# Every on-chip tile at a multiple of 128 bytes, in a kernel of two transformer blocks

## The chip, the cores and the metric

The kernel runs on one core of one Trainium2 chip. Times are device microseconds of one launch, the median of several runs. The core has TensorE (PE, matmuls and weight loads), VectorE (DVE), ScalarE (ACT), GpSimd (POOL) and SyncE (SP, which here issues the large loads), and an on-chip memory, SBUF, of 128 partitions. A tile occupies the same byte range of every partition, so "where a tile starts" is one number, its offset within a partition.

## The reference

Two blocks in a row on 272 tokens (16 meta tokens and 256) of width 2048, all in float32. What counts for the matmuls:

```
first block, x: 272 tokens
    proj = rms(h) @ w_in                           # 2048 -> rwkv, attention and gate columns
    y_a = rwkv7(...)    y_b = attention(...)       # 16 heads of 64 each, 1024 wide
    h = h + (g_a*(y_a@w_a) + g_b*(y_b@w_b)) @ w_o  # g: sigmoid of the gate columns
    gate, up = rms(h) @ w_gate_up                  # 5632 each
    h = h + (silu(gate)*up) @ w_down
second block, 256 tokens
    proj = rms(h) @ w_in_2
    y_hyena = x0 * long_conv(x1*v, filters)    y_attn = latent_attention(...)   # 1024 wide each
    h = h + rms([rms(y_hyena), rms(y_attn)] @ w_out)
    g, u = rms(h) @ w_up                           # 5632 each
    h = h + rms((gelu(conv3(g)) * u) @ w_down_2)
```

Past the mixer of the first block only the 256 real tokens are needed. The kernel multiplies transposed: weights are the stationary 128x128 block, and the tokens, 256 or 272 columns, the moving side.

## The kernel before

To keep float32 accuracy each float32 operand is split into two float32r parts, high and low, and each block product is three matmuls into one PSUM bank: high by high, low by high, high by low (`mm3`). `stream` brings a matrix in pieces of eight 128x128 blocks (512 KB): SP loads a piece to `wr`, ScalarE copies it to `wh` (L191), VectorE makes `wl = wr - wh` (L192). `wr`, `wh` and `wl` have three buffers each. `dense` then runs over the reduction steps k, with one piece in use and the next ones in preparation:

```
    def mm3(self, out, wh, wl, xh, xl, start, stop):
        nc.tensor.matmul(out, lhsT=wh, rhs=xh, start=start, stop=False)     # L209
        nc.tensor.matmul(out, lhsT=wl, rhs=xh, start=False, stop=False)     # L210
        nc.tensor.matmul(out, lhsT=wh, rhs=xl, start=False, stop=stop)      # L211

    def tl(self, pool, shape, tag, dt=F32, bufs=None):
        self.n += 1
        kw = {} if bufs is None else {"bufs": bufs}
        return pool.tile(list(shape), dt, tag=tag, name=f"{tag}_{self.n}", **kw)
```

The order of the work is the program's order, with the loads and splits of the weights brought forward; no instruction's place depends on addresses. The stages, and the moving side of each: w_in (tiles `xh`, `xl`: 16 rows of 272 tokens, 1088 bytes a row) with the heads' scans and attention between its blocks; w_ab (`ya`, `yb`); w_o (`mh`, `ml`); w_gu (`x2h`, `x2l`), 88 blocks of outputs by 16 steps; w_down (`hh`, `hl`), 16 blocks by 44 steps; the projections of the second mixer (`x3h`, `x3l`); w_out (`yhh`, `yhl`, `yah2`, `yal2`); w_up2 (`x4h`, `x4l`), 88 by 16; w_down2 (`hh2`, `hl2`), 16 by 44. All but w_in move 256 columns, rows of 1024 bytes.

All tiles come from pools that grow from the left end of a partition, or, with `side="right"`, from the right end down, each tile as long as its data. A pool opened first lies outermost. The left side begins with `g` (the columns of constants, `cols`, `con`, the token norms `R`, the sums `acc`) and `small` (the temporaries `rs_v`, `rs_r`, `rs_q`, `ssq`), then the weights; behind them the stage's input (`x2`, `x3`, `x4`, and in the first stage `xh`). On the right lie `h`, `mh`, then `hh`, and in the second block `yhh` and its like, then `hh2`.

Starts in bytes, as the program places them (one tile of each kind), and what is left over modulo 256:

```
tile                        before           after
wr, wh, wl (9 buffers)      28448 ...  32    28672 ...   0
x2h, x3h, x4h               65312      32    65536       0
x2l, x3l, x4l               81696      32    81920       0
xh (row k: + 1088 k)       106912     160   107520       0
mh                         180192     224   180096     128
hh, hh2                    122848,139232 224  (-96)    128
yhh                        194528     224   194432     128
rs_r, rs_q (mod 128)                 64, 0             0, 0
```

Buffers of the weights are 4096 bytes apart and their blocks 512, so all weights have the same remainder. Before, every SBUF tile starts at a multiple of 32 bytes, and 294 of 4267 at a multiple of 128.

Of the kernel before, what the change touches and what calls it, by code (L numbers as in the profile page):

```python
# [31 lines left out]
PIECE = 8  # L32

# [23 lines left out]
def in_order():  # L57
    """The column blocks of the first projection in the order in which they are computed."""
    out = [("wf", 0), ("ad", 0), ("gd", 0), ("gd", 1)]
    g = 0  # L60
    for j in range(9):
        if j < 8:
            out += [("k", j), ("v", j), ("r", j)]
        if j:
            out += [("fk", j - 1), ("fq", j - 1), ("fv", j - 1)]
        for _ in range(GATES_PER_PAIR[j]):
            out.append(("g", g))
            g += 1
    return out + [("g", i) for i in range(g, 32)]
# [18 lines left out]
def shape_constants():  # L88
    """Constants that depend on shapes alone."""
    p = np.arange(P)  # L90
    half = p // 64

    def pack(at, n, **vs):
        c = np.zeros((P, n), np.float32)
        for k, v in vs.items():
            s, w = at[k]
            c[:, s : s + w] = np.asarray(v, np.float32).reshape(P, w)
        return c

    z30 = np.zeros((P, 30))  # L100
    z30[p, 14 + half] = 1.0
    con = pack(CON, NCON, ident=np.eye(P), ones=np.ones((P, P)),
               bo=half[:, None] == half[None, :], i64=np.concatenate([np.eye(64)] * 2), z30=z30,
               eps=np.tile([[1e-6, 64e-5]], (P, 1)))

    s = np.arange(64)[:, None]
    t = np.arange(64)[None, :]
    g = np.stack([s < t, s <= t], 1)
    lv = np.stack([(s // (2 * b) == t // (2 * b)) & (s % (2 * b) < b) & (t % (2 * b) >= b)
                   for b in (1, 2, 4, 8, 16)], 1)  # L110
    sc = np.ones((P, L))
    sc[:, ::64] = 0.0
    crw = pack(CRW, NCRW, gmask=np.concatenate([g, g]), lev=np.concatenate([lv, lv]), scan=sc)

    ca = [np.where(np.arange(T)[None, :] > p[:, None] + NM + P * b, BIG, 0.0) for b in range(2)]
    cfx = pack(CFX, NCFX, caus=np.stack(ca, 1))

    pm = np.zeros((P, P))
    pm[half * 64 + (p + 32) % 64, p] = 1.0
    inv = (1.0 / (10000.0 ** (np.arange(0, 64, 2, dtype=np.float32) / np.float32(64)))).astype(np.float32)  # L120
    ang = (np.arange(S, dtype=np.float32)[:, None] * inv[None, :]).astype(np.float64)
    co, si = np.cos(ang).T, np.sin(ang).T
    cml = pack(CML, NCML, perm=pm, cos=np.concatenate([co] * 4), sin=np.concatenate([-si, si] * 2))

    n = 2 * S
    tt = np.arange(S, dtype=np.float64)
    ff = np.arange(S, dtype=np.float64)
    ph = 2.0 * np.pi * ((tt[:, None] * ff[None, :]) % n) / n
    alt = np.where(np.arange(S) % 2 == 0, 1.0, -1.0)
    re, im = np.cos(ph), -np.sin(ph)  # L130
    im[:, 0] = alt
    dft = np.concatenate([re, im], 1).reshape(2, P, 2 * S).transpose(1, 0, 2)
    ire, iim = np.cos(ph).T * (2.0 / n), -np.sin(ph).T * (2.0 / n)
    ire[0] /= 2.0
    iim[0] = alt / n
    idft = np.concatenate([ire, iim], 0).reshape(4, P, S).transpose(1, 0, 2)
    chy = pack(CHY, NCHY, dft=dft, idft=idft)

    f32 = np.float32
    pos = np.linspace(0.0, 1.0, S, dtype=f32)  # L140
    wv = (f32(2.0 * math.pi) * np.arange(S, dtype=f32) / f32(S)).astype(f32)
    fr = np.linspace(1e-4, 15, 16, dtype=f32)
    ang = (wv[:, None] * fr[None, :]).astype(f32)
    zp = np.concatenate([pos[:, None], np.cos(ang), -np.sin(ang)], 1).T
    dl = np.abs(np.linspace(math.log(1e-2) / 1.5, math.log(1e-2) / 0.3, 1024, dtype=f32))
    win = np.exp(-pos[:, None] * dl[None, :]) + f32(0.05)
    cfi = pack(CFI, NCFI, zpos=np.pad(zp, ((0, P - 33), (0, 0))), win=win.reshape(2, P, 1024).transpose(1, 0, 2))
    return {"con": con, "crw": crw, "cfx": cfx, "cml": cml, "chy": chy, "cfi": cfi}


class Builder:
    def __init__(self, nc, tc, a, o, upto, ctx):
        self.nc, self.tc, self.a, self.o, self.upto, self.ctx = nc, tc, a, o, upto, ctx
        self.n = 0
        self.nbank = 0
        self.banks = "dabc"
        self.pending = {}

# [9 lines left out]
    def tl(self, pool, shape, tag, dt=F32, bufs=None):  # L168
        self.n += 1
        kw = {} if bufs is None else {"bufs": bufs}  # L170
        return pool.tile(list(shape), dt, tag=tag, name=f"{tag}_{self.n}", **kw)
# [22 lines left out]
    def weights(self, src, kt, pools=None, size=PIECE, tag="w"):  # L194
        """Bring [128, kt, 128] weights on chip and split them into two float32r parts."""
# [10 lines left out]
    def mm3(self, out, wh, wl, xh, xl, start, stop):  # L206
        """out (PSUM) += (wh + wl)^T (xh + xl) without the product of the two low parts' last bits."""
# [5 lines left out]
    def stream(self, name):  # L213
        """The blocks [128, 128] of a matrix in the order of their use, PIECE at a time."""
# [6 lines left out]
    def dense(self, out, st, kt, xh, xl, tok):  # L221
        """out (PSUM) = sum over kt of w[p, kt, m]^T x[p, kt, tok]."""
# [4 lines left out]
    def group(self, out, st, kt, xh, xl, toks, bring):  # L227
        """Several blocks of outputs side by side: each block of x is used as soon as it is there."""
# [6 lines left out]
    def bank(self):  # L235
        """A bank for a block of outputs while no other work needs banks."""
# [3 lines left out]
    def gained(self, src, gain, hi, lo):  # L240
        """hi + lo = src * gain (a value for every partition)."""
# [3 lines left out]
    def sumsq(self, acc, src, first):  # L245
        """acc (+)= src^2, but for the last one added, which total() adds."""
# [10 lines left out]
    def total(self, acc, n=S):  # L257
        """The sums over the partitions of acc, on every partition (PSUM)."""
# [7 lines left out]
    def headsum(self, ps, w, src, n, pool=None):  # L266
        """ps = the sums of src over the 64 partitions of each head, weighted by w (exact in float32r)."""
# [7 lines left out]
    def warm_rsqrt(self, src):  # L275
        """Has the table of the reciprocal square root loaded ahead of its use."""
# [3 lines left out]
    def rstd(self, out, ss, n, scale, eps, floor=None, pool=None):  # L280
        """out = (scale * ss + eps)^-1/2 (ss in PSUM), refined by one Newton step."""
# [16 lines left out]
    def run(self):  # L298
        nc, tc, a, ctx = self.nc, self.tc, self.a, self.ctx
        g = self.g = self.pool(ctx, "g")  # L300
        self.small = self.pool(ctx, "small", 1)
# [88 lines left out]
    def residual(self, i, ps, gain, xh, xl):  # L390
        """h += ps; the next layer's input (but for the norm of each token) and its sum of squares."""
# [5 lines left out]
    def fox_setup(self, pr):  # L397
# [9 lines left out]
        # cumulative log forget gates  # L407
# [9 lines left out]
        # for each head of a pair: the high parts of the 16 heads' sums (and 16 unused rows), then the low ones  # L417
# [56 lines left out]
    def headnorm(self, ps, t0, w, w2, tag, gain):  # L474
        """RMS norm of each head (64 partitions) of ps * R."""
# [13 lines left out]
    def softmax(self, sc, mx, sign, w2):  # L489
        """sc = exp(sign * sc + mx) / its sum over the row, in place."""  # L490
# [63 lines left out]
    def conv3(self, ps, taps, bias, R, w2, tag):  # L554
        """Centred 3-tap convolution over the tokens of ps * R, plus bias."""
# [11 lines left out]
    def phase_mix(self, xh, xl, ys, rs):  # L567
# [3 lines left out]
        with ExitStack() as c:  # L571
            w = self.pool(c, "pmx")
            w2 = self.pool(c, "pmx2", 2)
# [21 lines left out]
            # latents of the queries and of the keys and values  # L595
# [22 lines left out]
            # queries [nope | rope], keys, and values (token-major) of all heads  # L618
# [61 lines left out]
    def transforms(self, w, jobs):  # L680
        """Split constant transform matrices into two float32r parts."""
# [5 lines left out]
    def filters(self, c):  # L687
        """The spectra of the implicit filters, in DRAM: a generator of steps."""
# [36 lines left out]
        for quarter in range(4):  # L725
# [17 lines left out]
            # [re 0, re 1, im 0, im 1, re 0 with the Nyquist term in its first row]  # L743
# [170 lines left out]
    def phase_x(self, pa):  # L914
# [4 lines left out]
        with ExitStack() as ph:  # L919
# [14 lines left out]
            # keep the tensor engine's clock up until the first data is there  # L934
# [6 lines left out]
            # the four blocks of the low-rank inputs and of the forget gates, while x comes in  # L941
# [20 lines left out]
    def lerp(self, ps, mu, t0, t1, out):  # L962
        """out = z + (z_prev - z) * mu for tokens t1.. of z = ps * R (ps holds tokens t0..)."""
# [11 lines left out]
    def phase_heads(self):  # L975
        """Projections of the first layer, its two kinds of heads, and the gates."""
# [4 lines left out]
        with ExitStack() as pr:  # L981
# [23 lines left out]
            # decay, rate and gate lora inputs  # L1005
# [43 lines left out]
    def rwkv_pair(self, j, w):  # L1049
# [7 lines left out]
        # decay exponents and rate  # L1057
# [13 lines left out]
        # the four scaled operands  # L1071
# [19 lines left out]
        # bonus term  # L1091
# [5 lines left out]
        # Gram blocks: rows (B s | K s), columns (A t | R t)  # L1097
# [15 lines left out]
        # values and (B | K) scaled to the end of the chunk, token-major  # L1113
# [19 lines left out]
        # X = (I - L)^-1 by doubling the size of the inverted diagonal blocks  # L1133
# [16 lines left out]
        for lv in range(1, 5):  # L1150
            # the first chunk has but 16 tokens
# [37 lines left out]
        # chunk after chunk  # L1189
# [33 lines left out]
        # group norm, bonus and gate  # L1223
# [21 lines left out]
def tiles_of(w):  # L1245
    """[K, M] -> [M / 128, 128, K / 128, 128], contiguous for every block of 128 columns."""
# [4 lines left out]
def stream_of(blocks):  # L1251
    """[n, KT, 128, 128] blocks in the order of their use -> [pieces, 128, PIECE, 128]."""
    return np.ascontiguousarray(blocks.reshape(-1, PIECE, P, P).transpose(0, 2, 1, 3))


def blocks_of(w):
    """[K, M] -> [M / 128, K / 128, 128, 128]"""
# [108 lines left out]
```

## Time and profile before

| | us |
|---|---|
| median of 3 runs | 2909.88 |
| lowest, highest | 2907.11, 2911.15 |
| profiled execution: span | 2911.4 |
| TensorE busy | 2864.9 (98%) |
| VectorE, ScalarE, GpSimd busy | 1863.8, 1337.1, 209.8 |
| mean granted TensorE clock | 0.993 |

The page gives the profiled execution its span alone; it lies 1.5 us above the median of the runs, which were taken apart from it, so the span is used as its time. In rows of groups, `out<-in` are the program's tiles, then partitions x elements, the count, the busy time and the mean of one in ns, and the idle time ahead with what ended it; a bank of PSUM is `psa` to `psd`, and the blocks of outputs go round the four, so a stage's matmuls stand in four times three rows. In rows of windows, stretch and length are followed by TensorE's busy time and its count of matmuls, the granted clock, and the DMA's share and rate. In rows of the timeline, the first column is the start and the second the duration in us.

### The profile page before, as it was taken

The page shows a single profiled execution, that of the slowest core. Times are in us where ns is not written, and L with a number is a line of the kernel's source. Part 1 is how long each engine was busy: PE and PEld are TensorE (multiplying, and loading weights), DVE is VectorE, ACT ScalarE, POOL GpSimd, SP SyncE. Part 2 cuts the span into 40 slices and gives each one's busy share as a digit, 9 for nine tenths or more (in the row PEclk, how much of TensorE's full clock was granted, in tenths as well). Part 3 has the DMA queues.
Part 4 walks back from the last instruction along what each step waited for, and adds up shares of the span by engine and source line. Part 5 has one row for each costly group of instructions (what it writes and reads, how often), then busy time and mean ns, then how long its engine had stood idle before and what let it go on. Part 6 is the DMA issues. An engine that isn't in the chain of part 4 may idle for free.

```text
span 2911.4 us, 58350 instructions
## 1 busy us (share of the span) xinstructions
PE 2864.9 (98%) x24314; PEld 2745.4 (94%) x24314; DVE 1863.8 (64%) x2958; ACT 1337.1 (46%) x1990; POOL 209.8 (7%) x358
## 2 busy tenths in 40 slices
PE   8999999999999999999999999999989999999997
PEld 7988888888989999999999999999989999999997
DVE  8856666766566655555555556687686666665445
ACT  6545555555434444444444445444454444444442
POOL 4000010000000200000000000010220000000001
PEclk9999999999999999999999999999999999999998
DMA  6433333334676555555556666444656655656664
GB/s 208 137 109 111 106 113 101 114 110 134 200 232 198 183 181 182 186 183 181 183 186 198 202 203 214 155 146 143 196 174 184 184 183 183 183 185 217 194 192 143
DMA packets 147481, 496.32 MB, mean 170 GB/s; under 512 B 16208, under 2 KB 30800, under 8 KB 146768
## 3 DMA queue, kind: packets, MB, share of 16 engines
q1 hardware_dynamic: 129024, 459.46, 50.2%
q10 hardware_dynamic: 17552, 31.03, 3.2%
q8 instruction: 190, 3.11, 0.4%
q0 software_dynamic: 640, 2.10, 0.2%
q14 instruction: 75, 0.61, 0.1%
HBM read 477.32 MB, written 15.20 MB: 169 GB/s over the span
## 4 chain that ended last, share of the span: by engine, by line
PE 96%; DVE 2%; DMA 1%; ACT 1%; issue 0%; SPq 0%; ACTq 0%; POOL 0%; DVEq 0%
PE psd L211 13%; PE psd L210 13%; PE psd L209 13%; PE psb L209 5%; PE psb L211 5%; PE psa L211 5%; PE psc L210 5%; PE psb L210 5%; PE psa L210 5%; PE psc L209 5%; PE psc L211 5%; PE psa L209 5%; PE psa L1107 1%; PE psa L1158 1%; PE psa L1164 1%; DMA fw<-filt_dram 1%
## 5 line engine op out<-in xcount | busy, mean ns | idle before, releaser
L192 DVE TENSOR_TENSOR wl<-wr,wh 128x1024 fp32r<-128x1024 f32 (+1 forms) x872 | 1066.6, 1224 | 665.0 <-ACT wh L191 664.0
L191 ACT CAST wh<-wr 128x1024 fp32r<-128x1024 f32 (+1 forms) x872 | 909.1, 1043 | 1256.5 <-PE psd L211 382.4
L210 PE MATMUL psd<-xh,wl 128*128 128x256 f32 (+2 forms) x1280 | 371.5, 290 | 0.0
L211 PE MATMUL psd<-xl,wh 128*128 128x256 f32 (+2 forms) x1280 | 371.4, 290 | 0.0
L209 PE MATMUL psd<-xh,wh 128*128 128x256 f32 (+2 forms) x1280 | 369.9, 289 | 0.6 <-DVE p L969 0.6
L209 PEld LDWEIGHTS psd<-xh,wh 128*128 128x128 f32 x1280 | 241.2, 188 | 8.6 <-issue 4.1
L211 PEld LDWEIGHTS psd<-xl,wh 128*128 128x128 f32 x1280 | 241.1, 188 | 7.8 <-issue 3.2
L210 PEld LDWEIGHTS psd<-xh,wl 128*128 128x128 f32 x1280 | 240.9, 188 | 5.3 <-issue 0.2
L252 POOL TENSOR_TENSOR acc<-acc,ssq 128x256 f32<-128x256 f32 x70 | 89.2, 1274 | 1103.8 <-ACT ssq L254 1103.7
L211 PE MATMUL psd<-x3l,wh 128*128 128x256 f32 x496 | 142.4, 287 | 0.0
L209 PE MATMUL psd<-x3h,wh 128*128 128x256 f32 x496 | 142.4, 287 | 0.0
L210 PE MATMUL psd<-x3h,wl 128*128 128x256 f32 x496 | 140.8, 284 | 0.0
L209 PE MATMUL psa<-x4h,wh 128*128 128x256 f32 x352 | 100.2, 285 | 3.8 <-ACT x4h L242 3.8
L210 PE MATMUL psa<-x4h,wl 128*128 128x256 f32 x352 | 100.4, 285 | 2.8 <-DVE wl L192 2.8
L211 PE MATMUL psa<-x4l,wh 128*128 128x256 f32 x352 | 100.4, 285 | 1.0 <-DVE x4l L243 0.6
L209 PE MATMUL psc<-x4h,wh 128*128 128x256 f32 x352 | 99.9, 284 | 0.0
L209 PE MATMUL psb<-x4h,wh 128*128 128x256 f32 x352 | 99.9, 284 | 0.0
L210 PE MATMUL psc<-x4h,wl 128*128 128x256 f32 x352 | 99.9, 284 | 0.0
L209 PE MATMUL psd<-x4h,wh 128*128 128x256 f32 x352 | 99.9, 284 | 0.0
L210 PE MATMUL psb<-x4h,wl 128*128 128x256 f32 x352 | 99.9, 284 | 0.0
L210 PE MATMUL psd<-x4h,wl 128*128 128x256 f32 x352 | 99.8, 284 | 0.0
L211 PE MATMUL psa<-x2l,wh 128*128 128x256 f32 x352 | 99.8, 284 | 0.0
(648 smaller groups left out, 8901.5 us busy)
## 6 DMA issues: line engine op xcount, KB each, us to landing
wr<-w_in_dram SPq DMA_DIRECT2D x230, 512.0 KB, 3.5
wr<-w_gu_dram SPq DMA_DIRECT2D x176, 512.0 KB, 3.5
wr<-w_down_dram SPq DMA_DIRECT2D x176, 512.0 KB, 4.2
wr<-w_up_dram SPq DMA_DIRECT2D x176, 512.0 KB, 3.6
wr<-w_ab_dram SPq DMA_DIRECT2D x32, 512.0 KB, 4.2
wr<-w_o_dram SPq DMA_DIRECT2D x32, 512.0 KB, 3.5
wr<-w_out_dram SPq DMA_DIRECT2D x32, 512.0 KB, 3.5
spill_g<-gate ACTq DMA_DIRECT2D x32, 128.0 KB, 2.7
```

What stands on the lines that cost most here:

```text
L191: self.nc.scalar.copy(hi, src)
L192: self.nc.vector.tensor_tensor(out=lo, in0=src, in1=hi.bitcast(F32), op=ALU.subtract)
L209: nc.tensor.matmul(out, lhsT=wh, rhs=xh, start=start, stop=False)
L210: nc.tensor.matmul(out, lhsT=wl, rhs=xh, start=False, stop=False)
L211: nc.tensor.matmul(out, lhsT=wh, rhs=xl, start=False, stop=stop)
L252: nc.gpsimd.tensor_tensor(out=acc, in0=acc, in1=self.pending[id(acc)], op=ALU.add)
L1107: nc.tensor.matmul(ps[:, c], lhsT=bk[hs, c0 + c], rhs=ar[hs, c0 + c], start=True, stop=True)
L1158: nc.tensor.matmul(ps[hs, c], lhsT=lm[hs, c], rhs=xn[hs, c], start=True, stop=True)
L1164: nc.tensor.matmul(ps[hs, c], lhsT=pp[hs, c], rhs=xt[hs, c], start=True, stop=True)
```

## The change

`tl`, which every SBUF tile but the pad goes through, rounds the last dimension (all free dimensions together) up to a multiple of 32 float32, 128 bytes, and hands out the part that was asked for. One pool of the hyena mixer, `pmx2`, is left as it was (`self.loose`). A pool `edge` of 96 bytes is opened first on the right side, so that tiles there end, and so begin, at a multiple of 128 instead of at 229344. Nothing reads or writes the pad. No instruction is added or taken away, and each engine's list has the same instructions in the same order with the same waits. Docstrings are blanked and a few lines are added, so line numbers move: L209 to L211 become L220 to L222, L191 and L192 become L202 and L203.

```
+LINE = 32
+EDGE = 24
...
+        self.loose = None
...
     def tl(self, pool, shape, tag, dt=F32, bufs=None):
         self.n += 1
         kw = {} if bufs is None else {"bufs": bufs}
-        return pool.tile(list(shape), dt, tag=tag, name=f"{tag}_{self.n}", **kw)
+        n = math.prod(shape[1:])
+        if n % LINE == 0 or pool is self.loose:
+            return pool.tile(list(shape), dt, tag=tag, name=f"{tag}_{self.n}", **kw)
+
+        t = pool.tile([shape[0], -(-n // LINE) * LINE], dt, tag=tag, name=f"{tag}_{self.n}", **kw)[:, :n]
+        if len(shape) == 2:
+            return t
+        names = "abcd"[: len(shape) - 1]
+        return t.rearrange(f"p ({' '.join(names)}) -> p {' '.join(names)}", **dict(zip(names, shape[1:])))
...
     def run(self):
         nc, tc, a, ctx = self.nc, self.tc, self.a, self.ctx
         g = self.g = self.pool(ctx, "g")
+
+        self.pool(ctx, "edge", side="right").tile([P, EDGE], F32, tag="edge", name="edge")
         self.small = self.pool(ctx, "small", 1)
...
-            w2 = self.pool(c, "pmx2", 2)
+            w2 = self.loose = self.pool(c, "pmx2", 2)
```

After it, 4184 of the 4267 tiles start at a multiple of 128 bytes; the others are in `pmx2` or are single columns.

## The prediction

> **What bounds the kernel now.** I read the head of the page and its slices first: who is busy, and whether evenly.
>
> ```profile
> span 2911.4 us, 58350 instructions
> PE 2864.9 (98%) x24314; PEld 2745.4 (94%) x24314; DVE 1863.8 (64%) x2958; ACT 1337.1 (46%) x1990; POOL 209.8 (7%) x358
> PE   8999999999999999999999999999989999999997
> PEclk9999999999999999999999999999999999999998
> PE 96%; DVE 2%; DMA 1%; ACT 1%; issue 0%; SPq 0%; ACTq 0%; POOL 0%; DVEq 0%
> ```
>
> The fourth line is the granted clock: full but for the edges. The last is the chain of work that ended last. TensorE is busy for 98% of the span, and its matmuls are 96% of the chain. So only two things can move the time by much: how far apart matmuls start, and, for the 2% that is left, the waits around them. The busy time is no measure of what one matmul costs, since consecutive ones overlap: a record lasts 0.28 us, and the next starts 0.12 us later.
>
> So the second view is the stages, each a window inside a stretch where TensorE never stops; its length over the count of matmuls is their spacing:
>
> ```profile
> core 0: us, PE busy (x), PEclk, DMA share, GB/s
> 753.00:798.00 45.00, 45.00 (x382) 1.00 0.70 227
> 961.00:1017.00 56.00, 56.00 (x477) 1.00 0.61 196
> 1030.00:1520.00 490.00, 490.00 (x4086) 1.00 0.58 183
> 1535.00:1760.00 225.00, 225.00 (x1988) 1.00 0.63 201
> 2062.00:2092.00 30.00, 30.00 (x257) 1.00 0.66 202
> 2400.00:2550.00 150.00, 150.00 (x1252) 1.00 0.59 183
> 2655.00:2885.00 230.00, 230.00 (x2032) 1.00 0.66 198
> ```
>
> In order these are the gates (w_in, moving side xh/xl), w_o (mh/ml), w_gu (x2), w_down (hh), w_out (yhh and its like), w_up2 (x4) and w_down2 (hh2). Every matmul in them has one shape, 128x128 weights by 256 float32r columns, at clock 1.00. Yet the spacings are 117.8, 117.4, **119.9**, **113.2**, 116.7, **119.8** and **113.2 ns**. DMA share and traffic don't order them (0.63 and 0.66 at the fast ones, 0.58 and 0.70 at slow ones). What does is where the operands lie, by the table of starts ahead of this text: the moving tiles of w_gu and w_up2 start at the same place modulo 256 bytes as the weights (both 32), those of w_down and w_down2 at 224, 64 bytes away. The switch can be watched on the timeline of TensorE where w_gu ends and w_down begins, with the same weight buffers going round:
>
> ```profile
> 1528.86 0.28 PE L211 MATMUL psd<-x2l,wh 128*128 128x256 f32 x1
> 1528.98 0.29 PE L209 MATMUL psa<-hh,wh 128*128 128x256 f32 x1
> 1529.10 0.28 PE L210 MATMUL psa<-hh,wl 128*128 128x256 f32 x1
> 1529.22 0.28 PE L211 MATMUL psa<-hl,wh 128*128 128x256 f32 x1
> 1529.34 0.28 PE L209 MATMUL psa<-hh,wh 128*128 128x256 f32 x1
> 1529.45 0.28 PE L210 MATMUL psa<-hh,wl 128*128 128x256 f32 x1
> 1529.56 0.28 PE L211 MATMUL psa<-hl,wh 128*128 128x256 f32 x1
> ```
>
> The starts (first column) are 0.12 us apart while x2 is read and for some four matmuls after, then 0.11. So in this kernel SBUF addresses do change TensorE's pace, by up to 6.7 ns of 120. The change is about addresses and nothing else, so this is the place to price it.
>
> [...] The stages agree that other engines' traffic doesn't set the spacing, but not that addresses are free: 113.2 against 119.9 ns for one shape. [...]
>
> **The change, part by part.**
>
> *Instructions.* None is added, removed or moved: each engine's list is the same, row for row, with the same waits. The pad at the right edge is 96 bytes that nothing writes or reads. So the whole cost lies in addresses.
>
> *Three kinds of place change.* (1) Absolute starts: nearly all from 32 or 96 past a multiple of 128 to 0. (2) The distance between moving operand and weights, modulo 256: it stays 0 for x2, x3, x4, y and hy; it goes from 64 to 128 for mh, hh, yhh and hh2, since the pad moves the right side by 96 bytes down and the weights move by 224 up. (3) xh and xl have rows of 1088 bytes, so the distance walks through 64, 0, 192, 128 with each k before; after, through the same four, two steps on.
>
> *w_down and w_down2, the large term.* 16 blocks of outputs by 44 steps by 3 matmuls, twice, is 4224. The count and the other large stages by shape:
>
> ```profile
> L209 PE MATMUL psa<-hh,wh 128*128 128x256 f32 x352 | 97.2, 276 | 0.0
> L209 PE MATMUL psd<-x2h,wh 128*128 128x256 f32 x352 | 99.6, 283 | 0.0
> L209 PE MATMUL psd<-x4h,wh 128*128 128x256 f32 x352 | 99.9, 284 | 0.0
> L211 PE MATMUL psd<-x3l,wh 128*128 128x256 f32 x496 | 142.4, 287 | 0.0
> L209 PE MATMUL psc<-mh,wh 128*128 128x256 f32 x64 | 18.0, 282 | 0.0
> L209 PE MATMUL psc<-yhh,wh 128*128 128x256 f32 x64 | 18.0, 281 | 0.0
> ```
>
> (352 times four banks times three products is 4224 for hh with hh2, and so for each of x2 and x4; x3 has 3 times 496; mh and yhh, with 16 blocks of 16 steps by 3, 768 each.) They lose distance 64, the one that gave 113.2 ns, and get 128. No long stretch of the trace stands at 128. Bounds: 113.2 if 128 serves as well as 64, so 0 us; 119.9 if it is no better than 0, so 4224 x 6.7 ns = +28.3 us. Nearest rows: the gates, whose k steps include one at 128 in every four, average 117.8, and one such step reads
>
> ```profile
> 776.25 0.28 PE L209 MATMUL psd<-xh,wh 128*128 128x256 f32 x1
> 776.36 0.28 PE L210 MATMUL psd<-xh,wl 128*128 128x256 f32 x1
> 776.49 0.28 PE L211 MATMUL psd<-xl,wh 128*128 128x256 f32 x1
> 776.60 0.28 PE L209 MATMUL psd<-xh,wh 128*128 128x256 f32 x1
> ```
>
> The first three are the step at 128: 0.35 us for three, some 117 ns each, with no sign of 113 (0.34). I take 117.8: 4224 x 4.6 ns = **+19.4 us**. All of it is on the path, since in these stages TensorE has no gap for it to hide in.
>
> *w_o and w_out.* Also 64 before, but at 117.4 and 116.7: distance 64 doesn't always give the fast pace. To 117.8: 768 x 0.4 + 768 x 1.1 = **+1.2 us**; bounds: 113.2, -5.9 us, and 119.9, +4.4 us.
>
> *w_gu, w_up2, x3 and the others with distance 0.* The distance is kept, so 0, if only the distance counts. Whether the absolute start counts, the trace shows at few places. The tiles of the small pool were at multiples of 64 already:
>
> ```profile
> 317.39 0.28 PE L272 MATMUL psb<-rs_r,bo 128*128 128x256 f32 x1
> 317.51 0.27 PE L436 MATMUL psb<-con,fv 128*128 128x128 f32 x1
> 375.05 0.31 PE L273 MATMUL psb<-rs_q,bo 128*128 128x320 f32 x1
> 375.20 0.28 PE L209 MATMUL psd<-xh,wh 128*128 128x256 f32 x1
> ```
>
> rs_r with the usual 256 columns keeps the next instruction away for 0.12 us, as x2 does, and rs_q (320 columns, at a multiple of 128) for 0.15 us, 0.47 ns a column like x2's 119.9/256. So a moving tile that begins on a line gains nothing by that. But these are single ones, and their weights weren't on a line. I take 0; the bounds are the first rival.
>
> *The gates and the rest of w_in.* The same four distances, so 0; if two of the four change their price, the bounds are those of the windows, 113.2 to 119.9 against 117.8.
>
> *Other engines.* VectorE's subtraction of the split (1224 ns a piece) and ScalarE's copy (1043 ns) read and write the moved tiles, and they are 64% and 46% busy behind TensorE. Aligned tiles that exist already show no gain:
>
> ```profile
> L254 ACT ACTIVATE ssq<-h 128x256 f32<-128x256 f32 x45 | 18.4, 410 | 0.0
> L191 ACT CAST hh<-glu_u 128x256 fp32r<-128x256 f32 x44 | 17.7, 403 | 0.0
> L192 DVE TENSOR_TENSOR wl<-wr,wh 128x1024 fp32r<-128x1024 f32 (+1 forms) x872 | 1066.6, 1224 | 665.0 <-ACT wh L191 664.0
> L191 ACT CAST wh<-wr 128x1024 fp32r<-128x1024 f32 (+1 forms) x872 | 909.1, 1043 | 1256.5 <-PE psd L211 382.4
> ```
>
> ssq, on a line, took 410 ns and hh, off it, 403. Zero, covered by the 1256.5 us that ScalarE waits, largely for TensorE to release buffers; were DVE a tenth slower, its 64% would still be cover.
>
> *DMA.* Pieces land in tiles now on a line. On the chain DMA has 1%, some 29 us; a tenth of it would be 3 us either way. I take 0.
>
> *Sum*: 19.4 + 1.2 = 20.6 us on the profiled execution's 2911.4 us span, so 2932.0. That execution stands 1.5 us above the median, 2909.88; I leave the difference in.
>
> **The rivals.**
>
> 1. *A start on a line is itself faster for weights and moving side.* Nothing measured has both on a line. If so, every stage reaches at least the pace seen in w_down: w_gu and w_up2 8448 x 6.7 = -56.6, x3 1488 x 6.7 = -10.0, w_o and w_out -5.9, w_in (about 3840 by 4.6) -17.7: -90, so **2821**. For it: 6.7 ns is much for a mere phase, and even 113.2 may carry a cost of straddling. Against: rs_r and rs_q. It decides from 2.5 ns a matmul on w_gu and w_up2 (8448 x 2.5 = 21), where it outweighs the loss at w_down. [...]
> 2. *128 is as far from 0 as it can be, so as good as 64 or better.* Then w_down keeps 113.2 and w_o and w_out come to it: -5.9 us, **2905**; each further ns on w_down is 4.2 us. For it: distance 0 is the worst seen. Against: the step at 776.25.
> 3. *The distance is not the cause* (what the tiles' side, or the length of the reduction, does to the pace stays), or 128 acts just like 64: **2911**. Against: the pace turned within a few matmuls with the tile.
> 4. *On a line operands collide more:* the distance-0 stages go up as well. 8448 + 1488 matmuls by 3 ns, half of the step seen, is +30 on top of 20.6: **2962**.
>
> **How the numbers follow.** The forecast 0.45 (its own range 2924 to 2943: w_down at 116 to 119.9, w_o and w_out to 119.9), rival 1 0.25, rival 2 0.12, rival 3 0.13, rival 4 0.05. A measurement here tells about 0.2%, 6 us, from no change. Slower: forecast and rival 4, 0.50. Rival 2 falls on the border, and I count it as faster with rival 1: 0.37. Same: 0.13. The range goes from somewhat below rival 1's time (2800: it has no exact floor) to 2948, past the forecast's upper bound; outside lie rival 4 and a rival 1 that is larger than the paces seen.
>
> **What would show it.** Right: the window over w_down has some 1910 matmuls where it had 1988, w_gu's stays near 120 ns, the counts and the chain stay. Wrong: w_gu and w_up2 under 117 ns (rival 1), w_down at 113 (2 or 3), w_gu over 121 (4). Most likely to undo it is that 128 in a steady run behaves otherwise than in the gates' walk, where each step inherits the state of the one before.

## The result, and the profile after

The changed kernel takes 2934.25 us (median of 4 runs, 2933.69 to 2935.81), the kernel before 2910.14 beside it (2907.11 to 2911.15): a ratio of 1.0086, with a 95% interval of 1.0074 to 1.0098. It is slower by 24 us; the forecast was 2932.0.

The page of the changed kernel, its head, slices of TensorE and the granted clock:

```profile
span 2932.5 us, 58350 instructions
PE 2887.7 (98%) x24314; PEld 2769.3 (94%) x24314; DVE 1863.2 (64%) x2958; ACT 1336.6 (46%) x1990; POOL 210.5 (7%) x358
PE   8999999999999999999999999999989999999997
PEclk9999999999999999999999999999999999999998
PE 96%; DVE 2%; DMA 1%; ACT 1%; issue 0%; POOL 0%; SPq 0%; DVEq 0%; ACTq 0%; POOLq 0%
```

Counts, clock and chain are those of before (mean granted clock 0.993, TensorE at 96% of the chain, both times). VectorE, ScalarE and GpSimd are busy for the same time within 0.7 us, so alignment gave them nothing and took nothing. TensorE alone grew, by 22.8 us of busy time. Where, the windows tell: the same stages as before (length, TensorE's busy time with the count of matmuls, clock, DMA share, GB/s), in order w_o, w_gu, w_down, w_out, w_up2, w_down2:

```profile
961.00:1017.00 56.00, 56.00 (x474) 1.00 0.58 183
1030.00:1520.00 490.00, 490.00 (x4086) 1.00 0.58 184
1535.00:1760.00 225.00, 225.00 (x1899) 1.00 0.59 192
2062.00:2092.00 30.00, 30.00 (x253) 1.00 0.65 218
2400.00:2550.00 150.00, 150.00 (x1252) 1.00 0.59 183
2670.00:2900.00 230.00, 230.00 (x1941) 1.00 0.61 188
```

w_gu and w_up2 have the same counts as before, 4086 and 1252, though all their operands now begin on a line (here and below a multiple of 128 bytes, the change's `LINE`, unless another length is given). w_down went from 1988 to 1899 matmuls in 225 us, w_down2 from 2032 in 230 to 1941. A window also counts the two or three matmuls that it cuts, so it reads a little short; from each start to that of the next matmul, over the whole stage (the mean of the differences under 160 ns, which leaves out true gaps), w_down and w_down2 go from 113.34 to **118.67 ns**, w_o from 117.46 to 118.66, w_out from 117.04 to 118.67, and w_gu stays at 120.00.

The timeline at the same place as before, from w_gu to w_down:

```profile
1526.10 0.28 PE L221 MATMUL psd<-x2h,wl 128*128 128x256 f32 x1
1526.22 0.28 PE L222 MATMUL psd<-x2l,wh 128*128 128x256 f32 x1
1526.34 0.28 PE L220 MATMUL psa<-hh,wh 128*128 128x256 f32 x1
1526.46 0.28 PE L221 MATMUL psa<-hh,wl 128*128 128x256 f32 x1
1526.58 0.28 PE L222 MATMUL psa<-hl,wh 128*128 128x256 f32 x1
1526.70 0.28 PE L220 MATMUL psa<-hh,wh 128*128 128x256 f32 x1
1526.82 0.28 PE L221 MATMUL psa<-hh,wl 128*128 128x256 f32 x1
1526.93 0.28 PE L222 MATMUL psa<-hl,wh 128*128 128x256 f32 x1
```

The step that followed the switch before, from 0.12 us a start to 0.11, no longer comes: the eight starts span 0.83 us, 0.119 each.

### The profile page after: what moved, and what is told of

Read it like the earlier page. It is cut to its first block, busy times and chain, and to the rows that moved or that the text cites. A ratio compares the mean times of both kernels' runs of the same rounds, so it can differ in the third digit from the quotient of the medians.

```text
span 2932.5 us, 58350 instructions
## 1 busy us (share of the span) xinstructions
PE 2887.7 (98%) x24314; PEld 2769.3 (94%) x24314; DVE 1863.2 (64%) x2958; ACT 1336.6 (46%) x1990; POOL 210.5 (7%) x358
## 4 chain that ended last, share of the span: by engine, by line
PE 96%; DVE 2%; DMA 1%; ACT 1%; issue 0%; POOL 0%; SPq 0%; DVEq 0%; ACTq 0%; POOLq 0%
PE psd L222 13%; PE psd L221 13%; PE psd L220 13%; PE psc L221 5%; PE psb L220 5%; PE psc L220 5%; PE psc L222 5%; PE psb L222 5%; PE psa L222 5%; PE psa L221 5%; PE psb L221 5%; PE psa L220 5%; PE psa L1120 1%; PE psa L1171 1%; PE psa L1177 1%; PE psc L1232 1%
## 5 line engine op out<-in xcount | busy, mean ns | idle before, releaser
L203 DVE TENSOR_TENSOR wl<-wr,wh 128x1024 fp32r<-128x1024 f32 (+1 forms) x872 | 1066.4, 1223 | 683.1 <-ACT wh L202 682.0
L202 ACT CAST wh<-wr 128x1024 fp32r<-128x1024 f32 (+1 forms) x872 | 908.4, 1042 | 1277.8 <-PE psd L222 390.1
L222 PE MATMUL psd<-xl,wh 128*128 128x256 f32 (+2 forms) x1280 | 371.5, 290 | 0.0
L220 PE MATMUL psd<-xh,wh 128*128 128x256 f32 (+2 forms) x1280 | 370.1, 289 | 0.6 <-DVE p L982 0.6
L220 PEld LDWEIGHTS psd<-xh,wh 128*128 128x128 f32 x1280 | 241.4, 189 | 8.6 <-issue 4.1
L222 PEld LDWEIGHTS psd<-xl,wh 128*128 128x128 f32 x1280 | 241.4, 189 | 7.8 <-issue 3.2
L220 PE MATMUL psd<-x3h,wh 128*128 128x256 f32 x496 | 142.6, 287 | 0.1
L222 PE MATMUL psd<-x3l,wh 128*128 128x256 f32 x496 | 142.5, 287 | 0.0
L220 PE MATMUL psa<-x4h,wh 128*128 128x256 f32 x352 | 100.3, 285 | 3.8 <-ACT x4h L253 3.8
L222 PE MATMUL psa<-x4l,wh 128*128 128x256 f32 x352 | 100.5, 286 | 1.1 <-DVE x4l L254 0.6
L220 PE MATMUL psb<-x4h,wh 128*128 128x256 f32 x352 | 100.0, 284 | 0.0
L222 PE MATMUL psa<-x2l,wh 128*128 128x256 f32 x352 | 99.9, 284 | 0.0
L220 PE MATMUL psa<-x2h,wh 128*128 128x256 f32 x352 | 99.9, 284 | 0.0
L222 PE MATMUL psd<-x4l,wh 128*128 128x256 f32 x352 | 99.9, 284 | 0.0
L220 PE MATMUL psd<-x4h,wh 128*128 128x256 f32 x352 | 99.8, 284 | 0.0
```

Source lines behind the costliest of these rows:

```text
L202: self.nc.scalar.copy(hi, src)
L203: self.nc.vector.tensor_tensor(out=lo, in0=src, in1=hi.bitcast(F32), op=ALU.subtract)
```

## The experiments

Below, "distance" is the start of the weights minus that of the moving tile, modulo 256 bytes. Spacings given to 0.01 ns are means of start-to-start differences, as above; in the sweeps they are taken from matmul 61 on, so that a stretch's first matmuls don't count.

### Is it the distance or the alignment?

Two kernels part what the change does together. The first keeps all padding and makes the pad at the edge 32 bytes instead of 96, so the right side stands at distance 64 again:

```
-EDGE = 24
+EDGE = 8
```

> All padding kept, so every tile stays on a multiple of 64 bytes, but the pad at the right edge is 32 bytes instead of 96: the right side starts at 192 modulo 256 and stands 64 bytes from the weights again, as in the kernel before. Theory, the distance between weights and moving side sets the pace: w_down and w_down2 go back from 118.7 to 113.3 ns a matmul (4224 x 5.4 = -22.8 us), w_o and w_out to about 117.3 (-2 us), total 2909 to 2912, the same as before. Rival, the absolute start (on or off a 128-byte line) sets it: the left side is as in the changed kernel and the right side is on a 64-byte line, so w_down stays near 118.7 and the total near 2934.

The second is the kernel before with 64 bytes at the right edge and no padded row: distance 128, with nothing aligned.

```
         g = self.g = self.pool(ctx, "g")
+        self.pool(ctx, "edge", side="right").tile([P, 16], F32, tag="edge", name="edge")
```

> The kernel before, without any row padding, with a pad of 64 bytes at the right edge alone: weights and all left tiles start at 32 modulo 256 as before, the right side at 160, so off any 64-byte line but 128 bytes from the weights, as in the changed kernel. Theory (distance): w_down and w_down2 at 118.7 ns, total 2932 to 2936. Rival (absolute start): nothing is aligned that was not, so w_down stays at 113.3 and the total at 2910.

The first took 2909.23 us, 1.0002 of the kernel before (0.9992 to 1.0011); the second 2935.85, 1.0095 (1.0078 to 1.0112). Windows of w_gu, w_down, w_out and w_down2 of the first, then w_gu and w_down of the second:

```profile
1030.00:1520.00 490.00, 490.00 (x4086) 1.00 0.58 184
1535.00:1760.00 225.00, 225.00 (x1988) 1.00 0.64 202
2062.00:2092.00 30.00, 30.00 (x267) 1.00 0.67 204
2655.00:2880.00 225.00, 225.00 (x1988) 1.00 0.65 193
```

```profile
1030.00:1520.00 490.00, 490.00 (x4086) 1.00 0.58 183
1535.00:1760.00 225.00, 225.00 (x1899) 1.00 0.61 192
```

All padding in place, and as fast as before; no padding but at the edge, and as slow as the change, to the matmul (1988 and 1899 in w_down). The first kernel alone wouldn't settle it, since its right side lies 64 bytes past a 128-byte line: with both sides on such lines only the distances 0 and 128 exist. The second does, being slow with nothing on a line that wasn't there before. So alignment shows neither a cost nor a gain of its own; what w_down lost goes with the distance.

One expectation missed. w_out was to stay near 117.3 ns at distance 64 and came to 113.53 (267 matmuls in its window, 257 in the kernel before), while w_o stayed at 117.46. So one stage at one distance can have two paces; the next kernels take this up.

A third kernel asks how much of the loss sits in w_down and w_down2: it is the changed kernel with the moving tiles of these two stages alone moved 16 bytes down, to distance 144 (why 144, the sweeps below say). `fars` makes one tile for the high and the low part, which begin 16 bytes in.

```
+    def fars(self, pool, k, tag, count):
+        n = k * S
+        self.n += 1
+        t = pool.tile([P, count * n + 8], F32R, tag=tag, name=f"{tag}_{self.n}")
+        return [t[:, 4 + i * n : 4 + i * n + n].rearrange("p (a b) -> p a b", a=k) for i in range(count)]
...
-                hh = self.tl(hp, [P, HT, S], "hh", F32R)
-                hl = self.tl(hp, [P, HT, S], "hl", F32R)
+                hh, hl = self.fars(hp, HT, "hh", 2)
```

(and so for hh2.)

> The changed kernel, with the two pairs of moving tiles of w_down and w_down2 alone put at 112 modulo 256 (144 bytes from the weights by weights minus moving side, a distance that gave 113.34 ns in all of four stretches of the sweeps); all else stays where the change put it. Theory (the change's loss sits in these 4224 matmuls): 4224 x (118.67 - 113.34) = -22.5 us from 2934, so 2911 to 2913, w_o and w_out staying at 118.7. Rival (the loss is spread, or came through the aligned loads and splits): 2920 to 2934.

It took 2913.5 us (1.0012 of before, 1.0002 to 1.0022), half a microsecond above the stretch expected, with w_down and w_down2 at 113.36 ns and w_o and w_out still at 118.65 and 118.66. So some 21 of the 24 us lie in these two stages. Of the 3 to 5 left, 2.2 are those of w_o and w_out by their spacings; the rest is within what the runs scatter.

### The left side at distance 64 as well

If distance 64 is good for w_down, it should be for the stages that stood at 0. This is the first kernel above, with 192 bytes between the weights and the left side's tiles:

```
 EDGE = 8
...
         self.wlo = self.pool(ctx, "wlo", 3)
+        self.pool(ctx, "gap").tile([P, 48], F32, tag="gap", name="gap")
```

> As the first kernel of this set (right side 64 bytes from the weights), and a pad of 192 bytes between the weights and the left side's tiles, so x2, x3, x4 and y of w_ab also stand 64 bytes from the weights, where they stood at 0. Theory (distance): w_gu and w_up2 go from 120.0 to 113.3 (8446 x 6.7 = -56 us), x3 -10, w_ab -5: 2840. The same with a state that depends on the length of the reduction (w_o and w_out, with 16 steps, ran at 117.3 at this distance, w_down with 44 at 113.3): 117.3, -28 us: 2882. Rival (the stage, not the distance): 120.0 stays, 2911.

2859.64 us (0.9831, 0.9776 to 0.9885), but the four runs were 2876.74, 2847.69, 2841.92 and 2871.59. The profiled one is the slowest of them. Its windows of w_gu, w_down, w_up2 and w_down2:

```profile
1030.00:1480.00 450.00, 450.00 (x3973) 1.00 0.62 194
1505.00:1730.00 225.00, 225.00 (x1988) 1.00 0.64 202
2400.00:2550.00 150.00, 150.00 (x1276) 1.00 0.60 187
2615.00:2845.00 230.00, 230.00 (x1956) 1.00 0.60 188
```

w_gu came to 113.37 ns, but w_up2, the same shape at the same distance with the same 16 steps, to 117.73, and w_down2 (117.78) fell from the pace that w_down kept (113.33). So distance 64 has two paces, and the length of the reduction doesn't choose between them: both expectations were half right. 6336 matmuls by 4.4 ns is 28 us; that would be most of the 35 between the fastest run and this one, if the fastest had the good pace there, which no profile shows.

The three traces with a stage at distance 64 (the kernel before, the first kernel above, this one) show when the pace is chosen. They hold 100 uninterrupted runs at this distance, in which at least 13 matmuls follow each other within 160 ns. From the seventh start on, each of them keeps one mean: 113.3 to 113.4 ns in 49, 117.7 to 117.8 in 51, and none goes over from one to the other. The pace is kept even from stage to stage, over 6305 starts from w_gu into w_down and 6145 from w_up2 into w_down2 here. So in these runs it is set where TensorE begins again after an interruption, or where an unbroken stream comes to this distance, as from w_gu into w_down of the kernel before. w_out's last 597 starts follow the same wait for VectorE's `wl` in the kernel before (0.53 us) and in the first kernel (0.56 us), and run at 117.8 and at 113.3. What in the restart decides is not shown.

### The sweeps

To see the distance by itself, the layers were left out and TensorE ran stretches of one shape from resident tiles. Each entry of the list has the starts of `wh`, `wl`, `xh` and `xl` in bytes and the number of steps in a group.

```
+SECTIONS = [(0, 0, d, d, 96) for d in range(0, 256, 16)]
+SECTIONS += [(32, 32, d, d, 96) for d in range(0, 256, 32)]
+SECTIONS += [(0, 0, d, d, 96) for d in range(240, -1, -16)]
...
+        for s, (wh, wl, xh, xl, group) in enumerate(SECTIONS):
+            ...
+            for i in range(96):
+                ...
+                self.mm3(ps, w[0][:, k], w[1][:, k], x[0][:, k], x[1][:, k], i % group == 0, (i + 1) % group == 0)
```

> The layers are left out: TensorE alone runs 55 stretches of 288 matmuls of the same shape (128x128 float32r weights, 256 columns, three products per step) from resident tiles, one stretch for each place of the moving tiles and the weights; ScalarE and VectorE do next to nothing and no weights are brought. Theory (distance): spacing by the distance modulo 256, 120.0 at 0, 118.7 at 128, 113.3 to 117.5 at 64, the same whether the weights start at 128 or at 160 modulo 256. Rival (absolute start): stretches with both sides on 64-byte lines fall apart from those at 32 past one, whatever the distance. Rival (other engines' traffic): without it all stretches run at one pace, 113 or less.

Windows of 25 us inside eight stretches, in order at distances 144, 128, 64, 0 (weights at 160 modulo 256), 128 (weights at 160), 64 again, 144 again and 0 (weights at 128):

```profile
259.00:284.00 25.00, 25.00 (x223) 1.00 0.01 1
293.00:318.00 25.00, 25.00 (x213) 1.00 0.01 1
429.00:454.00 25.00, 25.00 (x214) 1.00 0.01 1
599.00:624.00 25.00, 25.00 (x211) 1.00 0.01 1
736.00:761.00 25.00, 25.00 (x213) 1.00 0.00 1
940.00:965.00 25.00, 25.00 (x223) 1.00 0.00 1
1110.00:1135.00 25.00, 25.00 (x223) 1.00 0.01 1
1347.00:1372.00 25.00, 25.00 (x211) 1.00 0.01 1
```

Start to start: 120.00 at distance 0 and 118.64 to 118.69 at 128, both whether the weights begin at 128 or 160; 64 gives 117.78 when it follows 80 or 96, and 113.33 when it follows 48 or 0; 144 gives 113.33 both times. In groups of 16 steps instead of 96, 64 and 0 give the same 113.33 and 120.00. These are the paces of the kernel's stages to 0.03 ns, with the DMA at a share of 0.01 where the kernel has 0.6, and with VectorE and ScalarE busy for 2% and 1%. So the theory of the distance holds, and the rival of the other engines' traffic falls: w_gu's 120.00 comes from TensorE's own operands.

Four of the other stretches left all at distance 0 but for one tile, whose pairs stood at 64. Moving the low part of the weights, or the high part, gave 117.78 each, the low part of the moving side 117.78, its high part 119.27. A high part serves two of the three products. If each matmul had the pace of its own pair (113.33 at 64, 120.00 at 0), one product of three at 64 would give 117.78, and two would give 115.56, which didn't come. So paces of single pairs can't be added up, and a mixed sequence needn't tell what a long stretch at one distance will do.

The second sweep goes in steps of 4 bytes, all distances twice, in falling and in scattered order, with 192 matmuls each.

> As the first sweep (the layers left out, TensorE alone, resident tiles), with 192 matmuls a stretch and the moving tiles moved in steps of 4 bytes: all 64 distances in falling order, all 64 again in a scattered order, then 16 distances with 272 columns in rows of 1280 bytes. Theory (the distance sets the pace, at some distances with two paces by what ran before): 0 at 120.0 and 128 at 118.7 in both orders, 64 at 113.3 or 117.8, 144 at 113.3 in both orders; no distance under 113. Rival (the distance sets one pace, the two values came from the order of the stretches alone): each distance that gave two values gives one in each order, but 144 is then as likely to show 117 or more in the scattered order. [...]

Mean spacing in ns, first the falling order, then the scattered one:

```
distance   0        16       32       48       64       80       96       112
        120.0    117.1    118.3    119.2    113.3    119.3    117.3    113.3
        120.0    117.1    118.3    119.2    117.8    119.3    117.3    118.7
distance 128       144      160      176      192      208      224      240
        118.7    113.3    120.0    120.0    117.8    118.3    116.7    113.3
        118.7    113.3    120.0    118.3    117.8    118.3    116.7    116.7
```

Of the other 48, none is under 115.5, and the worst, 152, came to 130 in one order. So 144 is the only one of the 64 at 113.3 in both orders; 64, 112 and 240 show it in one. No distance goes under 113.3, those that are no multiple of 16 included. The 16 stretches of 272 columns at the end gave 125.3 ns at distance 0, 123.3 at 144, 160, 176 and 64, and up to 126.7 elsewhere, 128 among them.

### Every stage at distance 144

The changed kernel, with `fars` on the moving side of every large stage behind w_in (w_ab's y tiles get a 256-byte pad each instead), and 96 bytes of pad ahead of the left side's. For x2, and so for the others:

```
+                self.pool(pb, "gapx2").tile([P, 24], F32, tag="gap", name="gapx2")
                 xp = self.pool(pb, "x2")
-                xh = self.tl(xp, [P, KT, S], "x2h", F32R)
-                xl = self.tl(xp, [P, KT, S], "x2l", F32R)
+                xh, xl = self.fars(xp, KT, "x2", 2)
```

> The changed kernel with the moving tiles of every stage behind w_in (y of w_ab, m, x2, hh, x3, the second block's y, x4, hh2) at 112 modulo 256, so 144 bytes from the weights. Theory (144 has one pace, 113.34, whatever ran before): from the kernel before, w_gu and w_up2 -56, x3 -10, w_ab -5, w_o and w_out -6: 2830 to 2836, and runs that agree within some 3 us. Rival (144 too has two paces, as 64 has): 2840 to 2870, with runs far apart, as when all stood at 64 (2842 to 2877).

2840.55 us (2838.72 to 2840.97), a ratio of 0.9766 to the kernel before (0.9749 to 0.9784): faster than both kernels, and the runs agree. The windows of w_gu, w_down, w_up2 and w_down2:

```profile
1030.00:1480.00 450.00, 450.00 (x3973) 1.00 0.61 195
1500.00:1725.00 225.00, 225.00 (x1987) 1.00 0.64 201
2400.00:2550.00 150.00, 150.00 (x1326) 1.00 0.65 195
2585.00:2810.00 225.00, 225.00 (x1988) 1.00 0.64 196
```

All four run at 113.3 to 113.4 ns now. It is 4.6 us above the upper end expected. Part of it: stages with interruptions don't quite get there (x3 at 115.06, w_ab at 114.2, w_o at 113.77), which by their counts is 3.5 us; the rest I can't place. The trace shows what the interruptions do at this distance: after most of them the first 6 to 12 starts average 117.5 to 119 ns, and then the pace settles. All 41 uninterrupted runs of 24 starts or more are at 113.3 to 113.5 from the thirteenth on, so 144 does come to its one pace after every restart.

### Columns and weights of other sizes

> The layers left out again: stretches of 192 matmuls with 256 and with 512 columns and with weights of 128, 64 and 32 columns, at distances 0, 192, 144, 128, 64, 0, 128, 144 in this order. [...]

Windows at 256 columns, distances 0 and 144; at 512 columns, distances 64 and 0; and with weights of 64 columns and 256 moving ones, distances 0 and 144:

```profile
138.00:153.00 15.00, 15.00 (x128) 1.00 0.00 1
184.00:199.00 15.00, 15.00 (x133) 1.00 0.00 1
388.00:418.00 30.00, 30.00 (x130) 1.00 0.00 1
432.00:462.00 30.00, 30.00 (x134) 1.00 0.00 1
671.00:686.00 15.00, 15.00 (x135) 1.00 0.00 1
716.00:731.00 15.00, 15.00 (x131) 1.00 0.01 1
```

From start to start:

```
weights   moving   distance 0   144     128     64      192
128 cols  256      120.00     113.33  118.7   113.34  117.77
128       512      226.67     231.1   232-233 233.33  228.89
64        256      113.33     116.68  116.7   119.02  116.67
32        256      113.3-117.8 113.33 113-115.5 113.33 113.33
64        512      230.0      226.7-231.1 229.4-231.1 232.68 228.34
32        512      231.67     226.67  230.69  231.66  231.69
```

At 256 columns and weights of 128, distance 0 costs 6.67 ns more than 144 (120.00 and 113.33). If that came with each load of the weights, it would be the same at 512 columns and less with narrower weights; if it came with each column of the moving side, it would be 13.3 at 512 and the same with narrower weights. Neither holds. At 512 columns the order is turned round: 0 is best there with 226.67 and 64 worst with 233.33. With weights of 64 columns and 256 moving ones distance 0 falls to 113.33, but 144 rises to 116.68, so 0 is best there too; at 512 it isn't (230.0 against 226.66 in one of 144's two stretches). So these stretches show no good distance as such, only one for a shape; what makes it so they don't show, nor what a matmul would take without any such cost. One thing is the same in all: the lowest pace seen is 113.33 at 256 columns and 226.67, twice that, at 512, whether the weights have 128, 64 or 32 columns. So narrower weights didn't lower it.

## Why the prediction was right

**The mechanism.** It had the time within 2.3 us and for its reason: the change acts through the distance between weights and moving side, and through nothing else that the runs show. The kernel with 64 bytes at the edge alone (1899 matmuls in w_down's 225 us, as in the changed kernel) and the first sweep show it. In the sweep VectorE was busy for 2%, ScalarE for 1%, and the DMA had a share of 0.01 at most in the eight windows, yet the pace went from 113.3 to 120.0 with the distance of the two operands: where one lies relative to the other sets the pace.

**w_down and w_down2.** The one guess was the pace at distance 128, for which there was no long stretch. I took 117.8, the mean of the gates, and it is 118.67: 4224 x 5.33 = 22.5 us where the sum had 19.4. The bounds, 0 and 28.3, held it. The gates were a weak row for this. They change the distance every three matmuls, and from 753 us on their steps at 128 average 118.67 ns a matmul, but by the same rows 0 would cost 118.0 and 64 119.3, the reverse of the long stretches. That 128 came out near the mean of the gates is in part luck; the prediction named this as what was most likely to undo it. It also helped that 128 showed one pace in every long stretch of this shape (118.64 to 118.7), where 64 has two (113.33 and 117.78).

**w_o and w_out.** 2.2 us where the sum had 1.2, by the same pace.

**Distance kept, nothing changed.** w_gu, w_up2, x3 and w_ab stayed at 119.8 to 120.0, so the 0 was right. The two rows it was read from carried less than the prediction took from them: rs_r was 64 bytes past a line, and its 0.12 us is 116 ns in the trace, not x2's 120; rs_q alone was on a line, with 145 ns for 320 columns.

**w_in.** 118.00 to 117.91 with 256 columns, 125.74 to 125.81 with 272: the four distances in another order cost the same.

**The sum.** The stages give +24.7 us, the medians +24.1, the two profiled spans +21.1. The forecast was +20.6, so the step itself was 3.5 us too small. That the forecast time is nearer than that is luck: its base, 2911.4, was 1.3 us above the median of the runs beside the changed kernel. A run's time is also some 1.7 us longer than the span of the same execution (2934.23 and 2932.5), so the profiled execution of before was some 3 us slower than its median. Between the two profiles about that much fell away in waits elsewhere: w_ab, most of all, takes 2.6 us less from its first matmul to w_o's.

**The rivals.** Alignment as a gain: 0.00 ns at w_gu. 128 as good as 64: 118.67. No dependence on the distance: 5.3 ns. On-line operands that collide more: 120.00 as before. What the prediction had but didn't use is that w_o ran at 117.4 at the distance at which w_down ran at 113.3. It took this as "64 doesn't always give the fast pace" and went on; it was the sign that 64 has two paces. In the profiles of the kernel before and of the first kernel w_down and w_down2 have the good one, without anything that secures it.

## What to carry to other kernels

Where TensorE is the bound, as here (96% of the chain), compare the start-to-start spacing of matmuls of one shape between stages, not their durations. Here it was 120.00 ns in w_gu and 113.34 in w_down, at clock 1.00 and DMA shares of 0.58 and 0.63, and the step came from where the operands lie. Then sweep the distance between weights and moving tile for that shape, in both orders, and take one that is fast whatever ran before, as 144 was (113.3 in both orders): at 64 the pace came to 113.33 or 117.78 by how the stream started. Here moving the tiles to such a distance was worth 2.3%, while aligning everything to 128 bytes lost 0.9%. The number 144 itself is for 128x128 float32r weights and 256 columns; at 512 columns it is not the best (231.1 against 226.67 at distance 0).

## What the hardware showed that I had not expected

- At distance 64 TensorE runs at 113.33 or 117.78 ns and keeps the pace with which a stream starts until the next interruption (100 runs in three traces, none of which changes), over 6000 matmuls and more. The runs of one program between 2841.92 and 2876.74 us fit that, though only the slowest was profiled.
- Single steps of 4 bytes matter as much as steps of 64: 140 and 148 bytes have 121.7 and 120.0 beside 144's 113.3.
- The best distance for 256 columns (144, 64) is among the worse ones for 512 (231.1 and 233.3 against 226.67 at distance 0).
